# Two small tables of layer 0 in another pool: where the tiles of a matmul begin in the on-chip memory

## The chip, the cores and the metric

The kernel runs on one core of a Trainium2 chip. The metric is the device time of one execution in microseconds (us), lower being better; given is the median of three runs.

## The reference

Two layers of a diffusion backbone over 256 latent tokens and 256 context tokens, with 2048 channels and in float32. Layer 0 mixes tokens with centred pooling windows, layer 1 with neighbourhood attention, and a gated MLP with 5504 hidden channels follows each. Shift, scale and gate of every sub-layer come from a product of SiLU(c) with a table of 2 x 2048 x 12288 weights.

```python
for i in range(DEPTH):                       # 2 layers
    ml = (silu_c @ w_mod[i] + b_mod[i])      # six vectors for the latent tokens
    mc = (silu_cc @ w_mod[i] + b_mod[i])     # six for the context tokens
    a = modulate(rms_norm(h, norm1_g[i]), ml[0], ml[1])
    h = h + ml[2] * mixer_i(a)               # pooling (0), neighbourhood attention (1)
    u = modulate(rms_norm(h, norm2_g[i]), ml[3], ml[4])
    h = h + ml[5] * conv_ffn(u, w_gate, w_up, conv_w, conv_b, w_down)
# conv_ffn: gate = conv3(u @ w_gate); (silu(gate) * (u @ w_up)) @ w_down
```

Layer 0 does this for both streams, side by side as 512 columns; layer 1 needs its MLP for the latent stream alone.

## The kernel before, in words

Channels lie on the 128 partitions, tokens along the free axis. Activations and weights are each split into a high and a low part of a reduced float32 kind (`split`, L133 to L149), and a product is made of three matmuls, high by high, high by low and low by high, summed in a bank of PSUM. In layer 0 these are the lines L634, L635 and L636 for the gate and up projections (`gu0`) and L660, L661 and L662 for the down projection (`down0`). Each has a stationary operand of 128 x 128 (weights) and a moving one of 512 columns (activations of both streams).

Per hidden block f of 128 channels `gu0` runs a chain of 48 matmuls for g and one of 48 for u. After every four f, `down0` runs over a chunk of four hidden blocks: for each of four groups `wd_0` to `wd_3` of output channels 48 matmuls. `gu0` runs for f = 8 to 42, `down0` for eleven chunks, ten of four blocks and one of three; together these are 3360 and 2064 matmuls. They fill the stretch from about 437 to 1740 us. Beside them, VectorE, ScalarE and GpSimd split the next weights, take the banks of PSUM away, apply convolution and gate, and prepare the modulation of layer 1 (`mod_pairs`). The first eight hidden blocks' projections are made before 437 us, in pieces between the pooling mixer and the modulation.

The tiles that matter here, by pool:

- `main`, for the whole kernel: tables, the residual stream `hl`, and the modulation tables `modT`, 48 of 32 bytes a partition (layer by 24).
- `wst`: staging of loaded weights. `whp`: three pairs of split weights. `ap0`: sixteen tiles `A0` to `A15` for the split activations that the gate and up projections stream, and in layer 1 again.
- `p0`, for layer 0 only: the context stream `hc`, `quad` (512 bytes a partition, the weights of a small sum in `quarter_sum`, L167), `sc`, and `wsh` (128 bytes, corrections of the first eight blocks).
- `f0`, for layer 0 only: scratch tiles `t2` and the split hidden activations `act`, which the down projection streams. `whx`, for layer 0's MLP only: a fourth pair of split weights. `mp` behind it.

`split` takes the pools in turn, so every fourth half of a weight block comes from `whx` and the other three from `whp`:

```python
137            turn[0] += 1
138            pools = [whp] * 3 + extra
139            pool = pools[turn[0] % len(pools)]
```

In the built program `whx` holds the first half of every u block, and one half of the weights of two of the four groups of each down chunk (`wd_1` and `wd_3` in the chunk that starts at 569.94 us). The pools lie one behind another in the memory of a partition, so the size of `main` and `p0` decides where `f0`, `whx` and `mp` begin. Layer 1 opens its own pools where `p0` was.

Of the kernel before, what the change touches and what calls it, by code (L numbers as in the profile page):

```python
# [10 lines left out]
F32 = mybir.dt.float32  # L11
# [6 lines left out]
P = 128  # L18
# [12 lines left out]
NS = 8  # L31
# [28 lines left out]
def kernel(ctx: ExitStack, tc: tile.TileContext, xT, cxT, wmod, wg, wu, wd, wp,  # L60
                         wq, wv, wo, vec, cc, rope, inv, strips, out):
    nc = tc.nc
    main = ctx.enter_context(tc.tile_pool(name="main", bufs=1))
# [7 lines left out]
    def bank(tag, name):  # L71

        if tag == "d" and nbank[0] is not None:
            nbank[0] += 1
            if nbank[0] % 4 == 0:
                tag = "m"
        return pp.tile([P, 512], F32, tag=tag, bufs={"gu": 4, "d": 3, "m": 1}[tag], name=name)

    def flat(a):
        return a.rearrange("p s t -> p (s t)")  # L80
# [5 lines left out]
    def V(name):  # L86
        a, b = _OFF[name]
        return vt[:, a:b]
# [34 lines left out]
    def load(src, cols, name):  # L123

        ts = []
        for j in range(0, cols, 1024):
            n = min(1024, cols - j)
            t = stage(f"{name}_{j}")
            nc.sync.dma_start(t[:, :n], src(j, j + n))
            ts.append((t, n))  # L130
        return ts
# [23 lines left out]
    modT = {}  # L155

    both = (0, 1)

    def by_row(ps):

        return ps.rearrange("p (i j c) -> p i c j", i=4, j=4)[:, :, 0:2, :]
# [8 lines left out]

    def finish_mod(l, ch, streams, src):

        mt = src[0] if len(src) == 1 else main.tile([P, 4, 2], F32, name=f"modT{l}_{ch}")
        n = len(streams)
        which, q = divmod(ch, 4)

        def dup(name, a):
            return V(name)[:, a : a + 8].rearrange("p (i s) -> p i s", s=2)[:, :, 0:n]

        bias = dup(f"bm_{l}", 8 * ch)  # L180
        for b, v in enumerate(src):
            own = slice(32 * b, 32 * b + 32) if len(src) > 1 else slice(0, P)
            nc.vector.tensor_tensor(mt[own, :, 0:n], v, bias[own], op=ALU.add)
        if which in (1, 4):
            nc.vector.scalar_tensor_tensor(mt[:, :, 0:n], mt[:, :, 0:n], 1.0, dup(f"g{1 if which == 1 else 2}_{l}", 8 * q),
                                           op0=ALU.add, op1=ALU.mult)
        modT[l, ch] = mt

    def mod_pe(l, ch, sc, pool):

        ps = bank("m", f"mod{l}_{ch}")
        for g in range(4):
            ts = load(lambda a, b: wmod[l, ch, g, :, a:b], 2048, f"wm{l}_{ch}_{g}")
            for j in range(4):
                nc.tensor.matmul(ps[32 * j : 32 * j + 32, :], sc[:, 4 * g + j, :],  # L195
                                 ts[j // 2][0][:, 512 * (j % 2) : 512 * (j % 2) + 512],
                                 start=(g == 0), stop=(g == 3), tile_position=(0, 32 * j))
            if g == 3:
                ev = pool.tile([P, 512], F32, tag="t2", name=f"modev{l}_{ch}")
                nc.scalar.copy(ev, ps)  # L200
            yield
        with tc.high_priority():
            p2 = bank("d", f"modt{l}_{ch}")
            for i in range(4):
                nc.tensor.transpose(p2[:, P * i : P * i + P], ev[:, P * i : P * i + P], ident)
        r = main.tile([P, 4, 2], F32, name=f"modT{l}_{ch}")
        nc.vector.tensor_reduce(out=r, in_=by_row(p2), axis=AX.X, op=ALU.add)
        finish_mod(l, ch, both, [r])

    def mod_pairs(todo, ring):  # L210
# [20 lines left out]
        for i, (l, ch, m, streams, piece) in enumerate(steps):  # L231
            n = len(streams)
            while len(loaded) < min(i + 1 + ahead, len(steps)):
                fetch(*steps[len(loaded)])
            if piece == 0:
                acc = mp.tile([P, 1024], F32, tag="macc", bufs=1, name=f"macc_{l}_{ch}")
                acc = [acc, acc] if m == 2 else [acc[:, 0:512], acc[:, 512:1024]]
            for k, v in loaded[i]:
                for s in streams:
                    if k == 0:  # L240
                        nc.vector.tensor_scalar(acc[s], v, sc2[:, k, s : s + 1], None, op0=ALU.mult)
                    else:
                        nc.vector.scalar_tensor_tensor(acc[s], v, sc2[:, k, s : s + 1], acc[s],  # L243
                                                       op0=ALU.mult, op1=ALU.add)
            if ending is not None:
                ending()
                ending = None
            if piece == 8 * m - 1:
                r = mp.tile([P, 2, 16, 2], F32, tag="modr", bufs=2, name=f"modr_{l}_{ch}")
                for c in range(m):  # L250
                    for s in streams:
                        t = f0.tile([P, 512], F32, tag="t2", name=f"modu{s}_{l}_{ch}_{c}")
                        nc.vector.transpose(t, acc[s][:, 512 * c : 512 * c + 512])
                        nc.vector.tensor_reduce(out=r[:, c, :, s], in_=t.rearrange("p (k r) -> p k r", r=32),
                                                axis=AX.X, op=ALU.add)

                def ending(l=l, ch=ch, m=m, streams=streams, n=n, r=r):
                    for c in range(m):
                        finish_mod(l, ch + c, streams, quarter_sum(r[:, c, :, 0:n], n, f"modt_{l}_{ch + c}"))
            yield  # L260
# [64 lines left out]
    with ExitStack() as ph0:  # L325
        p0 = ph0.enter_context(tc.tile_pool(name="p0", bufs=1, reuse_waits="tile"))
        f0 = ph0.enter_context(tc.tile_pool(name="f0", bufs=6, reuse_waits="tile"))
        hc = p0.tile([P, KT, T], F32, name="hc")

        quad = p0.tile([P, 4, 32], F32, name="quad")  # L330
        nc.vector.tensor_reduce(out=quad[:, 0], in_=ident.rearrange("p (j c) -> p c j", j=4), axis=AX.X, op=ALU.add)
        for j in range(1, 4):
            nc.vector.tensor_copy(quad[:, j], quad[:, 0])
        quad = flat(quad)
# [8 lines left out]
        sc = p0.tile([P, KT, 32], F32, name="sc")  # L343
        nc.gpsimd.memset(sc, 0.0)
        nc.vector.tensor_copy(sc[:, :, 0:2], sc2)
        wsh = p0.tile([P, 2, NS, 2], F32, name="wsh")

        def late(f):

# [38 lines left out]
        with ExitStack() as phs:  # L388
# [32 lines left out]
            def mods():  # L421

                for g in range(4):
                    for w in (0, 1, 2, 4):
                        yield from mod_pe(0, 4 * w + g, sc, f0)
                    yield from mod_pe(0, 12 + g, sc, f0)
                    shifts(g)
                for q in range(4):
                    yield from mod_pe(0, 20 + q, sc, f0)
# [82 lines left out]
            def partial(g, sh, between):  # L512

                step = 0
                for fa in range(0, NS, 4):
                    for q, (nm, wsrc) in enumerate((("g", wg), ("u", wu))):
# [48 lines left out]
                        if g == 0:  # L565
                            nc.vector.tensor_reduce(out=w_, in_=by_row(p2), axis=AX.X, op=ALU.add)
                            continue
                        t_ = f0.tile([P, 512], F32, tag="t2", name=f"pu{nm}{g}_{fa}")[:, 0:8]
                        t_ = t_.rearrange("p (f s) -> p f s", s=2)
                        nc.vector.tensor_reduce(out=t_, in_=by_row(p2), axis=AX.X, op=ALU.add)  # L570
                        nc.vector.tensor_tensor(w_, w_, t_, op=ALU.add)
            lend(range(4, KT))
# [662 lines left out]
```

## Time and profile before

| what | us |
|---|---|
| median of three runs | 3086.99 |
| lowest and highest of them | 3086.82, 3088.39 |
| the profiled execution, its own time | 3084.26 |
| its span, first to last instruction | 3082.5 |
| TensorE busy (matmuls) | 3021.5 |

In the profile, PE stands for matmuls on TensorE, PEld for its loading of weights, DVE for VectorE, ACT for ScalarE, POOL for GpSimd, SP for the engine that issues the DMAs. Matmuls are pipelined: one is shown as lasting about 390 ns while the next starts some 230 ns after it. The step from start to start is therefore what a chain costs, and a difference in duration appears again in the step. A group's line gives the source line, engine, operation, tile written and tiles read, shape and count, and then busy us and mean ns of one.

### The profile page before, as it was taken

Reading aid. Unit: us, or ns where it says so; the run is one execution under the profiler, and the core shown is the slowest. Engines: PE = TensorE matmul, PEld = TensorE weight load, DVE = VectorE, ACT = ScalarE, POOL = GpSimd, SP = SyncE. Lnnn points to the kernel's source line nnn. Section 1 sums busy time; section 2 is a strip of 40 time slices with the busy share of each in tenths; the row PEclk is TensorE's granted clock in tenths of the full one; section 3 lists DMA queues with packets and bytes.
Section 4 is the critical chain, followed back from the end, with each engine's and each line's share of the span. In section 5 each row is a group of like instructions: output and inputs, shape, how many; then the busy total and the mean of one; then the engine's idle time right before and its main releaser. Section 6 shows DMA issues by size and latency. Waiting matters only on the chain.

```text
span 3082.5 us, 40828 instructions
## 1 busy us (share of the span) xinstructions
PE 3021.5 (98%) x15082; PEld 2411.2 (78%) x15082; DVE 1933.1 (63%) x2748; ACT 1373.2 (45%) x2219; POOL 828.8 (27%) x823
## 2 busy tenths in 40 slices
PE   6999999999999999999999999999999999999998
PEld 2565658888888888888887788878788888888887
DVE  4445764285674848557485665574777666666666
ACT  4333455323233332333324444343545666566665
POOL 2011313303022130312203000000002466556665
PEclk9999999999999999999999999999999999999999
DMA  9888562284755748465573233333345556555553
GB/s 386 331 276 308 206 233 96 89 254 139 222 175 181 222 144 250 139 215 185 170 237 105 98 109 110 103 114 98 116 150 189 180 184 198 192 186 183 183 193 117
DMA packets 177927, 559.70 MB, mean 182 GB/s; under 512 B 17600, under 2 KB 22208, under 8 KB 177728
## 3 DMA queue, kind: packets, MB, share of 16 engines
q1 hardware_dynamic: 177728, 557.10, 55.1%
q8 instruction: 119, 1.95, 0.2%
q14 instruction: 80, 0.66, 0.1%
HBM read 554.93 MB, written 2.10 MB: 181 GB/s over the span
## 4 chain that ended last, share of the span: by engine, by line
PE 94%; DVE 2%; DMA 1%; POOL 1%; ACT 1%; issue 1%; SPq 0%; DVEq 0%; ACTq 0%; POOLq 0%
PE g L769 5%; PE u L769 5%; PE d L660 5%; PE d L662 5%; PE d L661 5%; PE d L816 4%; PE u L634 4%; PE u L635 4%; PE u L636 4%; PE g L634 4%; PE g L636 4%; PE g L635 4%; PE mod L195 3%; PE u L772 3%; PE g L772 3%; PE d L820 2%
## 5 line engine op out<-in xcount | busy, mean ns | idle before, releaser
L673 POOL TENSOR_TENSOR hl<-hl,dy 128x256 f32<-128x256 f32 x160 | 149.6, 935 | 958.0 <-ACT dy L672 956.8
L831 POOL TENSOR_TENSOR hl<-hl,dy 128x256 f32<-128x256 f32 x320 | 331.6, 1071 | 188.3 <-ACT dy L829 186.1
L243 DVE SCALAR_TENSOR_TENSOR macc<-wm,sc,macc 128x512 f32<-128x512 f32 (+1 forms) x360 | 324.8, 933 | 68.1 <-DMA wm<-wmod 66.8
L672 ACT ACTIVATE dy<-d,modT 128x256 f32<-128x256 f32 x320 | 133.7, 470 | 195.6 <-PE d L662 195.6
L195 PE MATMUL mod<-wm,sc 128*32 128x512 f32 x768 | 132.3, 610 | 24.8 <-DMA wm<-wmod 24.8
L673 POOL TENSOR_TENSOR hc<-hc,dy 128x256 f32<-128x256 f32 x160 | 127.6, 797 | 0.0
L147 DVE TENSOR_TENSOR wd_2l<-wd,wd_2h 128x1024 fp32r<-128x1024 f32 (+1 forms) x44 | 54.2, 1235 | 112.7 <-ACT wd_2h L145 112.6
L829 ACT ACTIVATE dy<-d,modT 128x512 f32<-128x512 f32 x160 | 104.6, 685 | 42.9 <-PE d L820 41.4
L918 POOL TENSOR_TENSOR rk<-rk,rp 128x256 f32<-128x256 f32 x16 | 13.2, 827 | 365.6 <-DVE rk L917 309.9
L147 DVE TENSOR_TENSOR wd_3l<-wd,wd_3h 128x1024 fp32r<-128x1024 f32 (+1 forms) x44 | 52.0, 1202 | 80.2 <-ACT wd_3h L145 80.2
L147 DVE TENSOR_TENSOR wd_1l<-wd,wd_1h 128x1024 fp32r<-128x1024 f32 (+1 forms) x44 | 53.7, 1224 | 58.2 <-ACT wd_1h L145 58.2
L468 POOL TENSOR_TENSOR pf<-ws,inv 128x256 f32<-128x256 f32 x32 | 27.7, 887 | 223.4 <-DVE ws L463 150.7
L195 PEld LDWEIGHTS mod<-wm,sc 128*32 128x32 f32 x768 | 23.6, 109 | 80.3 <-issue 60.0
L147 DVE TENSOR_TENSOR wd_0l<-wd,wd_0h 128x1024 fp32r<-128x1024 f32 (+1 forms) x44 | 54.6, 1247 | 42.4 <-ACT wd_0h L145 42.4
L145 ACT CAST wd_1h<-wd 128x1024 fp32r<-128x1024 f32 (+1 forms) x44 | 45.2, 1029 | 80.6 <-PE u L635 55.7
L1007 ACT ACTIVATE sb<-sb,nm 128x512 f32<-128x512 f32 x64 | 46.1, 721 | 64.3 <-DVE nm L1003 63.1
L145 ACT CAST wd_0h<-wd 128x1024 fp32r<-128x1024 f32 (+1 forms) x44 | 45.3, 1031 | 59.9 <-PE g L635 30.2
L795 DVE TENSOR_TENSOR actb<-sgb,actb 128x256 fp32r<-128x256 f32 x43 | 52.4, 1218 | 26.7 <-ACT actb L794 26.7
L660 PE MATMUL d<-act,wd_2h 128*128 128x512 f32 x172 | 68.0, 395 | 0.0
L661 PE MATMUL d<-act,wd_2h 128*128 128x512 f32 x172 | 67.9, 395 | 0.0
L660 PE MATMUL d<-act,wd_3h 128*128 128x512 f32 x172 | 67.9, 395 | 0.0
L660 PE MATMUL d<-act,wd_0h 128*128 128x512 f32 x172 | 67.9, 395 | 0.0
(1752 smaller groups left out, 9276.3 us busy)
## 6 DMA issues: line engine op xcount, KB each, us to landing
wm<-wmod SPq DMA_DIRECT2D x384, 512.0 KB, 6.1
wd<-wd SPq DMA_DIRECT2D x168, 512.0 KB, 4.4
wg<-wg SPq DMA_DIRECT2D x156, 512.0 KB, 4.6
wu<-wu SPq DMA_DIRECT2D x156, 512.0 KB, 4.5
wv<-wv SPq DMA_DIRECT2D x32, 512.0 KB, 3.8
wk<-wq SPq DMA_DIRECT2D x32, 512.0 KB, 3.9
wq<-wq SPq DMA_DIRECT2D x32, 512.0 KB, 3.7
wo<-wo SPq DMA_DIRECT2D x32, 512.0 KB, 3.7
```

Source lines behind the costliest of these rows:

```text
L147: eng.tensor_tensor(lo[:, :n], t[:, :n], hi[:, :n].bitcast(F32), op=ALU.subtract)
L195: nc.tensor.matmul(ps[32 * j : 32 * j + 32, :], sc[:, 4 * g + j, :], ts[j // 2][0][:, 512 * (j % 2) : 512 * (j % 2) + 512], start=(g == 0) ...
L243: nc.vector.scalar_tensor_tensor(acc[s], v, sc2[:, k, s : s + 1], acc[s], op0=ALU.mult, op1=ALU.add)
L634: nc.tensor.matmul(ps, hi[:, c : c + P], xh, start=(k == 0), stop=False)
L635: nc.tensor.matmul(ps, hi[:, c : c + P], xl, start=False, stop=False)
L636: nc.tensor.matmul(ps, lo[:, c : c + P], xh, start=False, stop=(k == KT - 1))
L660: nc.tensor.matmul(ps, hi[:, o : o + P], xh, start=(i == 0), stop=False)
L661: nc.tensor.matmul(ps, hi[:, o : o + P], xl, start=False, stop=False)
L673: nc.gpsimd.tensor_tensor(h_of(s)[:, k, :], h_of(s)[:, k, :], y[:, s], op=ALU.add)
L769: nc.tensor.matmul(ps, hi[:, c : c + P], flat(B[k]), start=(k == 0), stop=False)
L772: nc.tensor.matmul(ps[:, T:], lo[:, c : c + P], B[k][:, 0], start=False, stop=(k == KT - 1))
L831: nc.gpsimd.tensor_tensor(hl[:, k, :], hl[:, k, :], y[:, q], op=ALU.add)
```

## The change

`quad` and `wsh` move from `p0` to `main`. To make room for them, twenty modulation tables of layer 0 (numbers 0 to 19) share their place with those of layer 1 that have the same number: 20 x 32 = 640 bytes, which is just the 512 + 128 that the two tables take.

```diff
+    def mod_tile(l, ch):
+
+        return main.tile([P, 4, 2], F32, tag=f"modT{ch if ch < 20 else (l, ch)}", name=f"modT{l}_{ch}")
+
...
-        mt = src[0] if len(src) == 1 else main.tile([P, 4, 2], F32, name=f"modT{l}_{ch}")
+        mt = src[0] if len(src) == 1 else mod_tile(l, ch)
...
-        r = main.tile([P, 4, 2], F32, name=f"modT{l}_{ch}")
+        r = mod_tile(l, ch)
...
-        quad = p0.tile([P, 4, 32], F32, name="quad")
+        quad = main.tile([P, 4, 32], F32, name="quad")
...
-        wsh = p0.tile([P, 2, NS, 2], F32, name="wsh")
+        wsh = main.tile([P, 2, NS, 2], F32, name="wsh")
```

In the built programs each engine has the same instructions in the same order with the same waits, before and after; only start addresses differ. Bytes within a partition, and what is left over 512:

| tiles | before | after | remainder before, after |
|---|---|---|---|
| `wst`, `whp`, `A0` to `A15` | 39424, 64000, 88576 and on | the same | 0, 0 |
| `t2` (six, of `f0`) | 175232 to 185472 | 174592 to 184832 | 128, 0 |
| `act` (seven of `f0`, one of `mp`) | 187520 to 224384 | 186880 to 223744 | 128, 0 |
| `whx` (high, low) | 216192, 220288 | 215552, 219648 | 128, 0 |
| `sc` | 171008 | 170496 | 0, 0 |
| `quad` | 170496 | 37824 | 0, 448 |
| `wsh` (no matmul reads it) | 173056 | 38336 | 0, 448 |
| `sh` (two, of the pooling stage) | 222592, 223104 | 221952, 222464 | 384, 256 |
| `ident`, `ones` | 20800, 20256 | the same | 320, 288 |
| all pools of attention and layer 1's MLP | | the same | mostly 0 |

## The prediction

> **What bounds the kernel now.** I read the profile page first, then the windows by stage, then the waits of TensorE in the stage that the change moves, and last single groups of matmuls there. From the page: the span, the busy time of TensorE, and the chain that ended last by engine.
>
> ```profile
> span 3082.5 us, 40828 instructions
> PE 3021.5 (98%) x15082; PEld 2411.2 (78%) x15082; DVE 1933.1 (63%) x2748; ACT 1373.2 (45%) x2219; POOL 828.8 (27%) x823
> PE 94%; DVE 2%; DMA 1%; POOL 1%; ACT 1%; issue 1%; SPq 0%; DVEq 0%; ACTq 0%; POOLq 0%
> ```
>
> TensorE is the bound: it is busy for 98% of the span and is 94% of the chain. The windows by stage (stretch: its length, then busy us and count of PE, PEld, DVE, ACT, POOL, granted clock, DMA share, GB/s) say where that is tightest.
>
> ```profile
> 0.00:437.00 437.00, 403.70 (x2180) 228.60 (x2180) 237.71 (x420) 175.54 (x331) 77.39 (x92) 1.00 0.82 299
> 437.00:1740.00 1303.00, 1296.11 (x5653) 1059.15 (x5653) 823.86 (x1080) 477.63 (x756) 273.14 (x325) 1.00 0.55 172
> ```
>
> From 437 to 1740 us, where layer 0's MLP runs, TensorE is busy for 1296.1 of 1303.0 us at the full granted clock. VectorE has 37% of the stretch free, the DMA engines 45%. The view of who waited for whom, for TensorE from 437 to 1690 us, has one line:
>
> ```profile
> PE g L634 <- DVE late L357: 0.9, 1, 0.9
> ```
>
> So in this stage there is no wait to take away, and no other engine holds TensorE back. Its length is the number of matmuls times the step from the start of one to the start of the next. The change alters no instruction, order or wait, only addresses; it can act on the time only if an address changes that step. So I look at groups that differ in nothing but the start address of an operand.
>
> First the rows of line L635 for block 11 (minimum, median and maximum of the duration in ns, then first and last start). The g chain has all its weights in whp; of the u chain the first half lies in whx, the second in whp. The moving tiles are the same A tiles in both.
>
> ```profile
> L635 PE MATMUL g<-A,wg_11h x16: 389/389/389, 548.2 to 558.4; 128*128 128x512 f32 x16
> L635 PE MATMUL u<-A,wu_11h x16: 389/391/404, 559.1 to 569.5; 128*128 128x512 f32 x16
> ```
>
> Then the groups of that u chain alone: the first row is from the window over its first half (558.90 to 564.48 us), the second from the window over the other half (564.49 to 569.93 us).
>
> ```profile
> L635 PE MATMUL u<-A,wu_11h 128*128 128x512 f32 x8 | 3.2, 395 | 0.0
> L635 PE MATMUL u<-A,wu_11h 128*128 128x512 f32 x8 | 3.1, 390 | 0.0
> ```
>
> Weights at remainder 128 (whx) against a moving tile at remainder 0 give 395 ns; both at 0 give 390 ns. In the down projection act is at 128, so there whp is the odd one and whx the equal one. Its groups over the whole stage:
>
> ```profile
> L661 PE MATMUL d<-act,wd_0h 128*128 128x512 f32 x172 | 67.9, 395 | 0.0
> L661 PE MATMUL d<-act,wd_1h 128*128 128x512 f32 x172 | 67.4, 392 | 0.0
> L661 PE MATMUL d<-act,wd_2h 128*128 128x512 f32 x172 | 67.9, 395 | 0.0
> L661 PE MATMUL d<-act,wd_3h 128*128 128x512 f32 x172 | 67.3, 391 | 0.0
> ```
>
> wd_0 and wd_2 come from whp alone: 395. wd_1 and wd_3 are half whx: 392 and 391, so their whx half takes about 2 x 391.5 - 395 = 388. The same pool is slow against A and fast against act. That speaks for the relation of the two remainders, and against whx being slow or fast in itself.
>
> **The change part by part.** Steps come from windows cut at the starts of chains, TensorE being busy throughout. In order: the g chain of block 11 (48 matmuls), the whx half of u (24), its whp half (24), then wd_0, wd_1, wd_2 and wd_3 (48 each).
>
> ```profile
> 548.01:558.90 10.89, 10.89 (x49) 9.01 (x48) 3.74 (x4) 2.71 (x4) 0.00 (x0) 1.00 0.33 96
> 558.90:564.49 5.59, 5.59 (x26) 4.53 (x24) 2.63 (x3) 2.36 (x4) 0.00 (x0) 1.00 0.33 98
> 564.49:569.94 5.45, 5.45 (x25) 4.50 (x24) 1.23 (x1) 1.04 (x2) 0.00 (x0) 1.00 0.31 96
> 569.94:581.13 11.19, 11.19 (x49) 9.01 (x48) 2.86 (x4) 5.15 (x10) 4.31 (x6) 1.00 0.14 47
> 581.13:592.22 11.09, 11.09 (x50) 9.03 (x48) 2.46 (x3) 5.36 (x11) 6.36 (x8) 1.00 0.32 96
> 592.22:603.38 11.16, 11.16 (x50) 9.04 (x48) 2.46 (x3) 5.36 (x11) 6.45 (x8) 1.00 0.28 95
> 603.38:614.47 11.09, 11.09 (x49) 9.03 (x48) 2.44 (x3) 5.35 (x11) 6.42 (x8) 1.00 0.29 95
> ```
>
> As steps: g 10.89 / 48 = 226.9 ns; u 5.59 / 24 = 232.9 and 5.45 / 24 = 227.1; wd_0 11.19 / 48 = 233.1; wd_1 11.09 / 48 = 231.0. After the change whp, whx, A and act all begin at remainder 0.
>
> *Up projection.* The whx half of u falls from 5.59 to 5.45 us, 0.14 us for each of 35 blocks: 4.9 us. The trace shows the target itself, in the second half of the same chain; I take it whole.
>
> *Down projection.* The chunk shown takes 11.19 + 11.09 + 11.16 + 11.09 = 44.53 us for 192 matmuls. The trace of before has no down chain with all operands at 0, so the new step is bounded from both sides. The best is the 227.1 of u: 43.60 us, a gain of 0.93. The least, if equal remainders pay at all, is the whx half of wd_1, with its changes between halves: 11.09 - 24 x 0.2331 = 5.50 us, 229.0 ns, 43.97 us, a gain of 0.56. There are ten chunks of four and one of three, 10.75 in all: 6.0 to 10.0 us. The nearest row in form is the pooling mixer, whose matmuls are laid out as in the down projection (three to a product, four channel blocks to a bank) with both tiles at 0:
>
> ```profile
> L487 PE MATMUL pm<-ph,wp2h x16: 389/389/389, 243.1 to 254.6; 128*128 128x512 f32 x16
> ```
>
> It never left 389, as the g chain never did. That draws me towards the better end, while the banks' changes and the sums for layer 1's modulation between the chains draw the other way: I take 228 ns, 43.78 us, 0.75 us a chunk, 8.1 us.
>
> *The rest.* The scratch tiles t2, quad and sh are read by small matmuls of the first stage and of the modulation; the two largest groups are:
>
> ```profile
> L205 PE MATMUL modt<-ident,modev 128*128 128x128 f32 x96 | 14.6, 275 | 5.9 <-ACT modev L200 5.9
> L530 PE MATMUL pwg<-wcg,sh 128*32 128x256 f32 x128 | 9.6, 384 | 1.6 <-ACT A L314 1.6
> ```
>
> No remainder here becomes equal or unequal in a way that the trace shows a price for. With the twin of the second line for u, 352 matmuls at most 6 ns either way are 2.1 us, in a stage in which TensorE idles 33 of 437 us and the DMA share is 0.82. I take nothing, and keep 2 us for the range. The shared modulation tables bring no new wait. The engines that must follow a faster TensorE have room (VectorE 63%), so I charge nothing for what is late next; if that cover went, the split weights on VectorE would be it.
>
> Sum: 4.9 + 8.1 = 13.0 us, bounds 10.9 and 14.9. On the profiled execution, 3084.3 - 13.0 = 3071.3; its time lies 2.7 us under the median of the runs shown, so for a median 3087.0 - 13.0 = **3074.0 us**.
>
> **The rivals.** *Only the up projection gains.* Layer 1's down projection has all tiles at remainder 0 already and yet shows no 389:
>
> ```profile
> L816 PE MATMUL d<-actb,wd_1h 128*128 128x512 f32 x160 | 43.7, 394 | 0.0
> L769 PE MATMUL g<-B,wg_2h x5: 389/395/398, 2370.5 to 2371.5; 128*128 128x512 f32 x5
> L769 PE MATMUL g<-B,wg_2h x5: 389/389/395, 2371.2 to 2372.1; 128*128 128x512 f32 x5
> ```
>
> If what makes 394 there also holds in layer 0's down projection, the gain is 4.9 us: 3082.1. Against it: in layer 1 matmuls of 512 columns follow runs of 256 columns, and the two rows of L769 (the first and the last five of one run of eight) show the median falling from 395 to 389 within the run. A run of four in L816 would end before that. Layer 0 has no such alternation. 12%.
>
> *The address is not the cause.* The Trainium skill ("SBUF — State Buffer", section "Who interferes with whom") gives TensorE two independent read ports, one for the moving operand and one for the weights, and says that it never waits for anyone; by that rule nothing here changes. In this kernel it would mean that the 0.14 us between the halves of u come from something else at that place, such as more work on VectorE and ScalarE (2.63 and 2.36 us against 1.23 and 1.04). The time would stay at 3087.0. Against it: wd_1 is faster than wd_0 though ScalarE and GpSimd do more beside it (5.36 and 6.36 against 5.15 and 4.31 us). So far the rows disagree with the rule's conclusion for the time. 6%.
>
> *Slower: equal remainders collide elsewhere.* t2 and act are also what the other engines read and write while TensorE streams A and whp; now they lie 128 bytes off, afterwards at the same remainder. If such accesses take turns with those of TensorE, the 2520 matmuls of the gate and up projections and about 520 of the down projection that are equal now would go from some 389 to layer 1's 394 ns, with the others staying where they are: 3040 x 5 ns = 15 us, 3102. For it: layer 1, where nearly everything is at 0, has 394. Against it: the explanation by runs above, and the pooling mixer, whose tiles are at 0 as well. It decides once the loss on these exceeds 13.0 / 3040 = 4.3 ns each. 8%.
>
> **How the numbers follow.** The forecast has 74%; it covers the bounds 10.9 to 14.9 us with 2 us for the rest and half a us for the runs. Its own range is 3069.5 to 3078.6. To take in the first rival, 3082.1, with a microsecond to spare, the range goes up to 3083.2; left out are the second and third, 14%, and a few per cent beyond the lower end. A measurement of this kernel tells 0.2%, 6.2 us, from no change. Faster by more: the forecast's 74% and the first rival's better part, 2%. Within it: the remaining 10% of the first rival and the 6% of the second. Slower: 8%.
>
> **What would show it right or wrong.** Right: the u rows at 389 to 390 as the g rows; the rows of L660 to L662 at 389 to 391 for all four groups, with no difference between wd_0 and wd_1; the chunk at 569.94 us at about 43.8 instead of 44.53 us; the stretch from 437 on shorter by 13 us, and the others unchanged. Wrong in size: L661 stays at 394 while u falls (first rival). Wrong altogether: whx and whp halves differ as now, or the g rows rise above 389.

## The result, and the profile after

The changed kernel takes 3070.64 us (median of four runs, 3068.39 to 3071.34) against 3087.69 us for the kernel before, measured beside it. The ratio is 0.9942 with a 95% interval of 0.9929 to 0.9954: 17 us less. The forecast was 3074.0 us, a gain of 13.

The page of the changed kernel, its span, busy times and chain by engine (lines after the change stand four further down: L634 is now L638, L661 is L665):

```profile
span 3068.5 us, 40828 instructions
PE 3007.0 (98%) x15082; PEld 2414.2 (79%) x15082; DVE 1939.4 (63%) x2748; ACT 1372.9 (45%) x2219; POOL 826.4 (27%) x823
PE 94%; DVE 2%; POOL 1%; DMA 1%; ACT 1%; issue 1%; SPq 0%; DVEq 0%; ACTq 0%; POOLq 0%
```

TensorE is the bound as before, and the 14 us that this span is shorter are 14.5 us of its busy time. The same number of matmuls took less. The windows over the same chains as in the prediction (g of block 11, the two halves of u, `wd_0` to `wd_3`):

```profile
547.59:558.47 10.88, 10.88 (x49) 9.02 (x48) 3.74 (x4) 2.69 (x4) 0.00 (x0) 1.00 0.33 96
558.47:563.91 5.44, 5.44 (x25) 4.51 (x24) 2.63 (x3) 2.36 (x4) 0.00 (x0) 1.00 0.33 99
563.91:569.35 5.44, 5.44 (x25) 4.51 (x24) 1.23 (x1) 1.06 (x2) 0.00 (x0) 1.00 0.34 98
569.35:580.23 10.88, 10.88 (x49) 9.01 (x48) 2.81 (x4) 5.14 (x10) 4.28 (x6) 1.00 0.16 48
580.23:591.11 10.88, 10.88 (x49) 9.02 (x48) 2.45 (x3) 5.36 (x11) 6.31 (x8) 1.00 0.31 98
591.11:601.99 10.88, 10.88 (x49) 9.01 (x48) 2.45 (x3) 5.36 (x11) 6.38 (x8) 1.00 0.30 97
601.99:612.87 10.88, 10.88 (x49) 9.02 (x48) 2.45 (x3) 5.36 (x11) 6.34 (x8) 1.00 0.29 96
```

Every chain of 48 takes 10.88 us now, 226.7 ns a step, whatever pool its weights came from: 5.44 us for both halves of u (before 5.59 and 5.45), 10.88 for each down group (before 11.19, 11.09, 11.16, 11.09). The work of VectorE, ScalarE and GpSimd beside them is what it was. The rows of one line each (minimum, median, maximum in ns, first and last start in us):

```profile
L639 PE MATMUL u<-A,wu_11h x16: 388/390/390, 558.7 to 568.9; 128*128 128x512 f32 x16
L665 PE MATMUL d<-act,wd_0h x172: 388/390/390, 460.8 to 1648.7; 128*128 128x512 f32 x172
L665 PE MATMUL d<-act,wd_1h x172: 388/389/390, 471.7 to 1656.9; 128*128 128x512 f32 x172
```

The maxima of 404 are gone. The first matmul of `wd_0` starts 1.0 us later than before and the last 15.5 us earlier (1664.2 before): 16.5 us between these two points alone.

### The profile page after: what moved, and what is told of

It reads as the page before. It is cut to its first block, busy times and chain, and to the rows that moved or that the text cites. A ratio compares the mean times of both kernels' runs of the same rounds, so it can differ in the third digit from the quotient of the medians.

```text
span 3068.5 us, 40828 instructions
## 1 busy us (share of the span) xinstructions
PE 3007.0 (98%) x15082; PEld 2414.2 (79%) x15082; DVE 1939.4 (63%) x2748; ACT 1372.9 (45%) x2219; POOL 826.4 (27%) x823
## 4 chain that ended last, share of the span: by engine, by line
PE 94%; DVE 2%; POOL 1%; DMA 1%; ACT 1%; issue 1%; SPq 0%; DVEq 0%; ACTq 0%; POOLq 0%
PE g L773 5%; PE u L773 5%; PE d L664 5%; PE d L666 5%; PE d L665 5%; PE d L820 4%; PE g L638 4%; PE g L640 4%; PE g L639 4%; PE u L639 4%; PE u L638 4%; PE u L640 4%; PE mod L199 3%; PE u L776 3%; PE g L776 3%; PE d L824 2%
## 5 line engine op out<-in xcount | busy, mean ns | idle before, releaser
L666 PE MATMUL d<-act,wd_2l 128*128 128x512 f32 x172 | 67.0, 390 | 0.0
L665 PE MATMUL d<-act,wd_2h 128*128 128x512 f32 x172 | 67.0, 390 | 0.0
L666 PE MATMUL d<-act,wd_3l 128*128 128x512 f32 x172 | 67.0, 390 | 0.0
```

What stands on the lines that cost most here:

```text
L665: nc.tensor.matmul(ps, hi[:, o : o + P], xl, start=False, stop=False)
L666: nc.tensor.matmul(ps, lo[:, o : o + P], xh, start=False, stop=(i == n - 1))
```

## The experiments

All but the ninth and the twelfth are the changed kernel with unused bytes put somewhere, so that tiles move and nothing else does: the instructions, their order and their waits are those of the changed kernel. Besides the time, the step counts: the mean from the start of one matmul to the next, from the trace, over the two projections of layer 0 (steps over 300 ns, which hold a gap, left out). Groups called equal have weights and moving tile at the same remainder.

**Theories.** A: the step depends on the distance between the starts of the weights and of the moving tile. B: each must itself begin at a multiple of 512. C: the moved tables, or the other engines' accesses to t2, are what counts.

**1. Act, whx and t2 back at 128.**

```diff
         wsh = main.tile([P, 2, NS, 2], F32, name="wsh")
+        p0.tile([P, 32], F32, name="gap")
```

> The changed kernel with 128 unused bytes behind sc in p0, so that t2, act and whx begin at remainder 128 again, while quad, wsh and the shared modulation tables stay where the change put them. If the remainders of act and whx against whp and A are the cause, all of the gain of 17 us goes: about 3087.5 us, u rows at 391 on average again, wd_0 at 395. If the moved tables (quad, wsh, the shared modT) were what paid, the time stays at 3070.6 us.

Measured: 3086.13 us, ratio to before 0.9997 (0.9987 to 1.0006). The whole gain is gone with the tables still moved. Groups of the down projection from 437 to 1690 us:

```profile
L666 PE MATMUL d<-act,wd_0h 128*128 128x512 f32 x172 | 67.9, 395 | 0.0
L666 PE MATMUL d<-act,wd_1h 128*128 128x512 f32 x172 | 67.4, 392 | 0.0
```

395 and 392, as before the change. The tables' part of C falls: they only made the room.

**2. Act, whx and t2 512 further.** As in the first, with 128 float32 (512 bytes).

> The changed kernel with 512 unused bytes in p0: t2, act and whx move by 512, so that their remainders modulo 512 are those of the changed kernel, modulo 1024 and above not. If 512 is the period, 3070.6 us with steps of 227 ns throughout. If the period is 1024 or more, the steps rise as far as in the kernel before: up to 3087.5 us.

Measured: 3069.06 us, ratio 0.9941 (0.9926 to 0.9956); steps 226.7 and 226.8 ns. No period above 512 is needed.

**3. All at 128.**

```diff
     hl = main.tile([P, KT, T], F32, name="hl")
+    main.tile([P, 32], F32, name="gapm")
```

> The changed kernel with 128 unused bytes in main: every tile behind it (wst, whp, A, act, whx, t2 and the pools of layer 1) begins at remainder 128, so all are equal and none is at 0. If the two operands' relation counts, 3070.6 us and 227 ns a step. If each operand must itself begin at a multiple of 512, all 5424 matmuls of layer 0's MLP pay some 6 ns, 32 us: above 3100 us.

Measured: 3072.14 us, ratio 0.9945 (0.9930 to 0.9960). The up projection for block 11, every operand at remainder 128:

```profile
L640 PE MATMUL u<-A,wu_11h x16: 389/389/389, 558.1 to 568.3; 128*128 128x512 f32 x16
```

and its groups of the down projection from 437 to 1690 us:

```profile
L666 PE MATMUL d<-act,wd_0h 128*128 128x512 f32 x172 | 66.9, 389 | 0.0
```

The steps are 226.7 and 226.8 ns. B falls: none of the tiles that these matmuls read begins at a multiple of 512 here, and the steps are the short ones.

**4. Only t2 back at 128.** 128 unused bytes in `p0`, and 384 in `f0` behind t2, so that act and whx are at 0.

> The changed kernel with t2 alone back at remainder 128 (128 unused bytes before it, 384 behind it), act and whx at 0. t2 is written and read by VectorE, ScalarE and GpSimd, and by TensorE in small transposes only. If the cause lies between the two operands of the matmuls, 3070.6 us. If it lies in the other engines' accesses beside TensorE, part or all of the 17 us comes back.

Measured: 3070.43 us, ratio 0.9943 (0.9928 to 0.9958); steps 226.7 and 226.8 ns. The place of t2, which VectorE, ScalarE and GpSimd read and write, shows no part in the time. C falls.

**5. Only act at 128.** 128 unused bytes in `f0` behind t2, and 384 more in a pool of their own ahead of `whx`.

> The changed kernel with the act tiles of f0 (seven of eight) at remainder 128, whx and all else at 0: the moving operand of the down projection is unequal to all its weights. By the relation of the operands, some 1800 to 2064 matmuls pay 6 ns: 11 to 12 us more than the changed kernel, 3082 us, with L664 to L666 at 395 in all four groups and the u rows at 389 to 390. If whx is what counts, 3070.6 us.

Measured: 3084.23 us, ratio 0.9988 (0.9978 to 0.9997), 13.6 us over the changed kernel where 11 to 12 were expected. Its groups of the down projection from 437 to 1690 us:

```profile
L668 PE MATMUL d<-act,wd_0h 128*128 128x512 f32 x172 | 67.9, 395 | 0.0
L668 PE MATMUL d<-act,wd_1h 128*128 128x512 f32 x172 | 68.0, 395 | 0.0
```

and its row of the up projection for block 11:

```profile
L642 PE MATMUL u<-A,wu_11h x16: 388/390/390, 561.2 to 571.4; 128*128 128x512 f32 x16
```

All four groups now pay, those with half their weights in whx too, and u does not.

**6. Only whx at 128.** 128 unused bytes in a pool ahead of `whx` and act's eighth tile kept in place by another 384 in one behind it, so only the fourth pair of weights moves; the 128 and 384 are

```diff
+        gp = ph0.enter_context(tc.tile_pool(name="gp", bufs=1, reuse_waits="tile"))
+        gp.tile([P, 32], F32, name="gapx")
         whx = ph0.enter_context(tc.tile_pool(name="whx", bufs=1, reuse_waits="tile"))
+        gq = ph0.enter_context(tc.tile_pool(name="gq", bufs=1, reuse_waits="tile"))
+        gq.tile([P, 96], F32, name="gapy")
```

> The changed kernel with whx alone at remainder 128: the stationary operand of half of each u chain (840 matmuls) and of a quarter of the down projection (about 520) is unequal to what streams. By the relation, 840 x 5.8 ns = 4.9 us and 520 x 6 = 3.1 us: 3078.6 us; u rows at 391 on average, wd_1 and wd_3 (half whx) slower than wd_0 and wd_2, which is the other way round from the kernel before. If the place of whx is slow or fast in itself, the down projection does not follow.

Measured: 3080.03 us, ratio 0.9972 (0.9962 to 0.9983). Its row of the up projection for block 11:

```profile
L643 PE MATMUL u<-A,wu_11h x16: 388/392/405, 558.8 to 569.2; 128*128 128x512 f32 x16
```

and its groups of the down projection from 437 to 1690 us:

```profile
L669 PE MATMUL d<-act,wd_0h 128*128 128x512 f32 x172 | 67.0, 390 | 0.0
L669 PE MATMUL d<-act,wd_1h 128*128 128x512 f32 x172 | 67.3, 391 | 0.0
```

The order of the groups is turned round: `wd_1`, half in whx, was the faster one before the change and is the slower one here. The rows of one line differ by 1 ns only; over all three lines of a product the steps are 226.8 ns for `wd_0` and 230.5 for `wd_1`, where before the change they were 233.1 and 231.0. whx is not slow or fast in itself. The unequal steps are 232.9 (up) and 232.8 ns (down). The equal chains beside them take 227.2 and 227.3 instead of 226.9 and 226.7: the cost spills a little over.

Where it spills can be read at the ends of the whx half. The timeline at its start, from g to u of block 11 (start, length, operation):

```profile
558.12 0.39 PE L643 MATMUL g<-A,wg_11h 128*128 128x512 f32 x1
558.34 0.40 PE L644 MATMUL g<-A,wg_11l 128*128 128x512 f32 x1
558.58 0.41 PE L642 MATMUL u<-A,wu_11h 128*128 128x512 f32 x1
558.82 0.40 PE L643 MATMUL u<-A,wu_11h 128*128 128x512 f32 x1
```

The step from the last matmul of g to the first of u is already long, 232.3 ns on the mean of the 35 blocks against 226.7 in the changed kernel. The stream and the weights of that matmul of g are equal; unequal are the weights of u, whose loading starts 4 ns after that matmul's own start (558.347 and 558.343 us in the trace). Behind the half, three steps between equal operands are still long, 228.6, 232.5 and 230.9 ns, and the next is 226.7.

**7 and 8. Act, whx and t2 at 256, and at 64.** As the first, with 64 and with 16 float32.

> The changed kernel with 256 unused bytes in p0: t2, act and whx at remainder 256. If 512 is the period and any difference costs alike, about 3087 us as with 128. If the period is 256, 3070.6 us.

Measured: 3068.80 us, ratio 0.9938 (0.9923 to 0.9953). The row of the up projection for block 11:

```profile
L640 PE MATMUL u<-A,wu_11h x16: 388/390/390, 558.5 to 568.7; 128*128 128x512 f32 x16
```

and its groups of the down projection from 437 to 1690 us:

```profile
L666 PE MATMUL d<-act,wd_0h 128*128 128x512 f32 x172 | 67.0, 390 | 0.0
```

A distance of 256 costs nothing. The period is 256 and not 512, over which the remainders above are taken: of the two branches, the second came true.

> The changed kernel with 64 unused bytes in p0: t2, act and whx at remainder 64. If any difference costs alike, about 3087 us; if the period is 64, 3070.6 us; if the cost grows with the distance, in between.

Measured: 3080.16 us, ratio 0.9973 (0.9962 to 0.9985), 9.5 us over the changed kernel, where 128 cost 15.5 in run 1. But not by a smaller price for each: the unequal up projection pays 233.2 ns in full, the down projection 229.1 on the mean. There it does not fall on the three lines of a product evenly, as the groups show:

```profile
L665 PE MATMUL d<-act,wd_0h 128*128 128x512 f32 x172 | 67.8, 394 | 0.0
L666 PE MATMUL d<-act,wd_0h 128*128 128x512 f32 x172 | 66.9, 389 | 0.0
L666 PE MATMUL d<-act,wd_2h 128*128 128x512 f32 x172 | 67.7, 394 | 0.0
L667 PE MATMUL d<-act,wd_2l 128*128 128x512 f32 x172 | 66.8, 388 | 0.0
```

By L666 alone `wd_0` would pay nothing and `wd_2` nearly all. Over the three lines they pay alike: their steps are 229.3 and 228.9 ns. So the row of a single line does not tell what a group pays.

The weights are 64 ahead of the moving tile in the up projection and 64 behind it in the down projection, so the sign seemed to count.

**9. One word of the change.**

```diff
-        wsh = p0.tile([P, 2, NS, 2], F32, name="wsh")
+        wsh = main.tile([P, 2, NS, 2], F32, name="wsh")
```

> The kernel before with one word changed: wsh in main instead of p0. main grows by 128 and p0 shrinks by 128, so wst, whp and A move to remainder 128 while t2, act and whx stay at 128: all equal, none at 0, quad still in p0 and no modulation table shared. By the relation of the operands this alone brings the whole gain: 3070.6 us, steps of 227 ns. If moving quad or sharing tables had a part, less.

Measured: 3069.28 us, ratio to before 0.9941 (0.9929 to 0.9954). Its row of the up projection for block 11:

```profile
L635 PE MATMUL u<-A,wu_11h x16: 389/389/389, 557.8 to 568.0; 128*128 128x512 f32 x16
```

and its groups of the down projection from 437 to 1690 us:

```profile
L661 PE MATMUL d<-act,wd_0h 128*128 128x512 f32 x172 | 66.9, 389 | 0.0
```

Made on the kernel before, this alone brings the whole gain. Neither quad's move nor the shared modulation tables are needed. It is not told apart in time from the changed kernel.

**10 and 11. At 192, and at 32.** As the first, with 48 and with 8 float32.

> The changed kernel with 192 unused bytes in p0: t2, act and whx at remainder 192. With 64 bytes the up projection's unequal half took 233.2 ns a step (weights 64 ahead of the moving tile) and the down projection's unequal matmuls 229.1 (weights 64 behind). If the period is 256 and the sign counts, 192 ahead is 64 behind: the two change places, 229 and 233 ns, together 1531 x 6.4 + 840 x 2.3 ns = 11.7 us and the half nanosecond of the neighbours, 3083 us. If the sign does not count and 64 is simply cheaper than 128 on the whole, 3080 us.

Measured: 3085.32 us, ratio 0.9993 (0.9984 to 1.0002). The two did change places: 228.9 ns up, 233.3 ns down. The time came out 2 us over the 3083 expected; what I had not counted are the equal whx matmuls of the down projection, which between unequal ones take 231.1 ns (528 x 4.4 = 2.3 us). A row of the up projection for block 11 and a group of the down projection from 437 to 1690 us:

```profile
L640 PE MATMUL u<-A,wu_11h x16: 389/392/394, 559.8 to 570.0; 128*128 128x512 f32 x16
L666 PE MATMUL d<-act,wd_0h 128*128 128x512 f32 x172 | 67.8, 394 | 0.0
```

> The changed kernel with 32 unused bytes in p0: t2, act and whx at remainder 32. If the cost falls with the distance, under the 9.5 us that 64 bytes cost: 3072 to 3078 us. If any difference inside 256 costs about the same, 3080 us or more. If the period were 32 or less, 64 could not have cost anything, so 3070.6 us would mean a threshold between 32 and 64.

Measured: 3089.54 us, ratio 1.0006 (0.9997 to 1.0016). The smallest distance tried costs the most: 233.1 ns up, 233.5 down. The cost does not grow with distance. The same two rows:

```profile
L640 PE MATMUL u<-A,wu_11h x16: 389/390/396, 560.6 to 571.0; 128*128 128x512 f32 x16
L666 PE MATMUL d<-act,wd_0h 128*128 128x512 f32 x172 | 67.9, 395 | 0.0
```

The mean steps of the unequal groups, by the distance of the weights ahead of the moving tile modulo 256:

| distance | up projection | down projection |
|---|---|---|
| 0 (changed kernel, 2, 3, 4, 7, 9) | 226.7 to 226.9 | 226.7 |
| 32 | 233.1 (run 11) | |
| 64 | 233.2 (run 8) | 233.3 (run 10) |
| 128 | 232.9 (before, 1, 6) | 232.8 (before, 1, 6), 233.1 (5) |
| 192 | 228.9 (run 10) | 229.1 (run 8) |
| 224 | | 233.5 (run 11) |

Where both projections have a value they agree, though they stream different tiles in chains of different length. That supports the distance modulo 256 as the variable, with one cheap value at 192.

**12. Layer 1 in longer runs.** This tests why layer 1's rows show 394 at equal remainders, on which the first and third rivals of the prediction rested. Its gate and up chain takes all sixteen high parts, then all sixteen low ones:

```diff
-                for j in range(2):
-                    hi, lo = parts[j]
-                    for k in range(8 * j, 8 * j + 8):
+                for k in range(KT):
...
-                        nc.tensor.matmul(ps, hi[:, c : c + P], flat(B[k]), start=(k == 0), stop=False)
+                    nc.tensor.matmul(ps, parts[k // 8][0][:, c : c + P], flat(B[k]), start=(k == 0), stop=False)
...
```

> The changed kernel with the gate and up projections of layer 1 in another order: sixteen matmuls of 512 columns, then sixteen of 256, instead of twice eight and eight. If the first matmuls of 512 columns after a run of 256 pay some 28 ns a run in all, as the steps 233, 236, 228, 233, 231, 227, 227 of a run suggest, half of the 172 runs go: 2.4 us less, 3068 us, and the step mean of L773 falls from 231.8 to about 229.5. If the steps over 227 in layer 1 come from something else, L773 keeps its mean and the time stays at 3070.6 us; a wait for split weights that arrive later would make it longer.

Measured: 3069.49 us, ratio to before 0.9941 (0.9929 to 0.9954), not told apart from the changed kernel. The timelines of the chain g of block 3 (start, length of the piece, operation, count), of the changed kernel:

```profile
2364.90 2.00 PE L773 MATMUL g<-B,wg_3h 128*128 128x512 f32 x8
2366.74 1.12 PE L776 MATMUL g<-B,wg_3l 128*128 128x256 f32 x8
2367.69 2.00 PE L773 MATMUL g<-B,wg_3h 128*128 128x512 f32 x8
```

and its row of that chain:

```profile
L773 PE MATMUL g<-B,wg_3h x16: 389/392/398, 2364.9 to 2369.3; 128*128 128x512 f32 x16
```

The timeline of the same chain in this kernel:

```profile
2367.72 3.82 PE L771 MATMUL g<-B,wg_3h 128*128 128x512 f32 x16
2371.37 2.08 PE L774 MATMUL g<-B,wg_3l 128*128 128x256 f32 x16
2373.29 3.82 PE L771 MATMUL u<-B,wu_3h 128*128 128x512 f32 x16
```

and its row of that chain:

```profile
L771 PE MATMUL g<-B,wg_3h x16: 389/389/398, 2367.7 to 2371.1; 128*128 128x512 f32 x16
```

The median falls from 392 to 389. The median steps by place in the chain say why: 233, 236, 228, 232, 231 and then 227, at the start of each run after matmuls of 256 columns. In the longer run the pattern comes once and the ninth to sixteenth step are all 227, though the same tiles are read there. So the long steps of these chains belong to the change of shape and not to addresses. For layer 1's down projection (L816 of the kernel before, 394 ns), which this run leaves as it was, that is an inference. The step mean of the line of 512 columns falls from 230.3 to 228.7 ns, 1.6 of the 2.3 ns expected. It is worth little: the chain takes 5.57 us (2367.72 to 2373.29) instead of 5.59.

## Why the prediction was right, point by point

*What bounds the kernel* held: the stretch has no waits, so each nanosecond off a step came out of the time. Between the same two matmuls before and after that stretch (the 2181st and the 7561st of the trace) 1231.9 us became 1215.1.

*The up projection*: 840 x (232.9 - 226.7) = 5.2 us for the 4.9 forecast.

*The down projection* is the term that was mis-sized: 8.1 us forecast from a step of 228 ns, bounds 6.0 to 10.0. The step became 226.7: 1536 x (232.8 - 226.7) = 9.4 us, and the quarter that was equal already came down from 229.2, 528 x 2.5 = 1.3 us more, 10.7 in all; the chunk takes 43.52 us now, where 43.78 was forecast. I had taken the middle between 227.1 and 229.0 because of bank changes and sums between the chains. These cost nothing that the step of 226.7 shows; the 229.0 was itself the trace of unequal neighbours, as run 6 shows, where the down projection's equal groups take 227.3. The 227.1 of u, which gave the upper bound, was such a trace too, so that 10.7 lies above the bound of 10.0. And the 388 ns for the whx half of `wd_1` were read off one line of three; its step before the change was 229.2, not below the 227 of the g chain.

*The equal chains of the up projection* I took as unchanged. They fell from 227.3 to 226.9 (0.47 before rounding): 2520 x 0.47 = 1.2 us. Together 5.2 + 10.7 + 1.2 = 17.1 us; the medians differ by 17.05. So the direction and the mechanism were right, but the gain lies above the bounds of the sum, 10.9 to 14.9. That the time still fell into the forecast's own range is owed to the 2 us kept for something else, the small matmuls of the first stage, and in that part it was luck.

*The rest* at nothing held within the scatter: from the 101st to the 301st matmul the changed kernel's profiled execution took 51.1 us against 49.7, and behind the 7561st 1405.0 against 1403.3. The profiled executions of runs 1 to 12 lie between 49.6 and 52.4 and between 1403.2 and 1406.4 there. The profiled execution of before lay 2.7 us under its median and that of after 0.3 under its own; so the two spans differ by only 14 us.

*The rivals.* That only the up projection gains: refuted by the rows of L665, and its ground, as far as the gate and up chains of layer 1 go, by run 12. That addresses are not the cause: refuted by runs 1, 5 and 6, where nothing but addresses differs. The Trainium skill ("SBUF — State Buffer", section "Who interferes with whom") gives TensorE two independent read ports and says that it never waits on anyone. As far as other engines go, run 4 agrees: t2's place changed nothing (3070.43 us). The conclusion that addresses leave the time alone does not hold here: with nothing but start addresses changed, the step went from 226.7 to 232.8 ns (run 6), and the measurement decides. That equal remainders collide with other engines: refuted by the g chains, which never rose.

*What stays open.* The runs show that the distance between a chain's weights and its moving tile sets the step. Why it does so they do not tell. The long step at the end of g in run 6 points to the weights that are loaded while the matmul before them streams, since there nothing else is unequal. But in runs 8 and 10 the same step is 225.8 and 225.9 ns, not longer than 226.7, so this is not settled. Open is also why 192 is cheap, and why in run 8 the extra falls on one line of a product more than on another.

## What to carry to other kernels

When TensorE has no waits left, compare rows of the same matmul that differ only in the pool of one operand: here a few nanoseconds a step on 2400 matmuls were 17 us. Place stationary and moving tiles of float32 matmuls of this form at a distance that is a multiple of 256 bytes; it is the distance and not the absolute place that counts, and a small table of odd size ahead of a large pool is enough to spoil it. Count the steps over a whole chain, since the row of one line can show none of the extra or all of it. Look for the smallest move that does it: one word did as much as the whole change.

## What the runs showed of the hardware that was not expected

The period is 256 bytes and the cost is not graded: 32 bytes off costs 6.3 to 6.8 ns a step, as much as 128, and 192 only 2.2 to 2.4. Equal chains in the neighbourhood of unequal ones pay as well (227.3 against 226.7 to 226.9, and up to 231.1 in run 10). And the first five matmuls of 512 columns after a run of 256 take up to 9 ns more each, with all remainders equal. The steps behind an unequal half of u, from its last matmul on (235.9, 228.6, 232.5, 230.9, then 226.7 ns in run 6), are nearly those after a run of 256 columns from the second on (236, 228, 232, 231, then 227); why, no run tells.
